# Sums of squares of the norms on TensorE: one column of ones as moving operand instead of 128

## The chip, the core and the metric

The kernel runs on one core of one Trainium2 chip, as one launch. The metric is the device time of that launch in microseconds (us). A core has five engines that work beside one another, each through its own instructions in their order: TensorE (PE, matrix products; the loading of its stationary operand is shown apart as PEld), VectorE (DVE), ScalarE (ACT), GpSimd (POOL) and SyncE (SP, which here only issues DMA transfers). They wait for one another through semaphores.

## The reference, cut to what matters

Two transformer layers over 512 tokens `x` and 256 context tokens `ctx`, of 1024 channels, and a last norm. Every norm is an RMS norm; the attention of layer 0 has one per head as well (`diff_out`).

```python
def rmsnorm(x, g):
    xf = x.astype(jnp.float32)
    y = xf * lax.rsqrt(jnp.mean(xf * xf, axis=-1, keepdims=True) + EPS)
    return (y * g.astype(jnp.float32)).astype(x.dtype)

def modulate(x, g, shift, scale):
    return rmsnorm(x, g) * (1 + scale) + shift

def diff_out(o, g, lam_init):
    b, t = o.shape[0], o.shape[1]
    return (rmsnorm(o, g) * (1.0 - lam_init)).reshape(b, t, B_V_WIDTH)

# reference(), one layer l
    a = modulate(h, norm1_g[l], sh1, sc1)
    ac = modulate(hc, norm1_g[l], csh1, csc1)
    ...                                      # l = 0: even_mixer, l = 1: odd_mixer
    h = h + g1 * y
    h = h + g2 * swiglu(modulate(h, norm2_g[l], sh2, sc2), ffn_w_in[l], ffn_w_out[l])
    ...                                      # the same for hc in layer 0
    return rmsnorm(h, final_g)
```

## The kernel before

**Layout.** Activations are kept transposed: eight tiles of 128 channels by tokens. Almost all time goes into large products, which are computed in three passes of a high and a low part (`mm3`, L106 to L108). A matmul of fp32 operands, as the norms use it, is shown as two records in the trace, each with its own weight load: two passes.

**One norm.** `squares` (L186) and code like it squares the channel tiles on ACT (L191) and adds them up on DVE (L193) to a tile `sq` of 128 partitions by T tokens, whose column sums are wanted. In the feed-forward parts some of the squares aren't added beforehand: they are handed over as a list `more` of further tiles (`sqs`), and TensorE adds them. `rstd_diag` (L145) then does the following.

- For each block of 128 tokens a matmul with the block of `sq` as the stationary operand (128 by 128) and `ones`, a 128 by 128 tile of ones, as the moving one (L156); for each tile of `more` the same again, added in PSUM (L161). Row p of the result is the sum of token p; all its 128 columns are equal.
- DVE reads one column of each block with a stride of 128 (`col`), scales it and adds EPS (L164, or L166 in the heads), and works out the reciprocal root in ten small instructions, L135 to L139, on 128 by 2 to 128 by 6 values.
- DVE writes for each block a diagonal matrix of these values (L173).

`spread` (L179) multiplies ones with the diagonals (L183), which puts the value of each token on all 128 partitions; DVE and ACT then modulate the activations with it (L199 to L201 in `modulate`).

**Where it is called.** At the start for `x` (four blocks), in the first projections for `ctx` (two blocks), in the four heads of layer 0's attention (`norm`, four and two blocks in each), before and within both feed-forward parts (`ffn_rstd` and `ffn`), before layer 1 for both streams (`modulated`, four and two blocks with four tiles of `more`), and at the end in two halves (`final_rows`, two blocks with three tiles of `more` each). In all there are 94 sum matmuls: 50 at L156 and 44 at L161, or 188 passes.

**The order of the work.** The program is written in Python as a sequence, and the framework's scheduler (`TileContext(..., schedule_with_timeline_sim=True)`, the last lines of the file) places the instructions of each engine by its own estimates of how long each takes. A different operand size can therefore move instructions that have nothing to do with the norms.

**Names of the places.** In the attention of layer 0, `qa`, `qb`, `kh` and `kl` are a head's queries and keys, `pw` their products in PSUM (L542, L543), `e` the exponentials (ACT, L546), `pb` from L564 their transposes, `ath` and `atl` the high and low part of these (L122, L123), which are multiplied with the values `vhi` and `vlo` by L106 to L108. Matmuls to `pf` from `ax` and a weight slot `w` are the gated projections of the other branch, which fill TensorE's time between. For layer 1, `w` is a weight slot: ACT writes its high part (L81) and POOL the low part (L84); `ax` are the high (ACT, L200) and low (DVE, L201) part of the normed activations; `pw` their product.

Of the kernel before, what the change touches and what calls it, by code (L numbers as in the profile page):

```python
# [14 lines left out]
P = 128  # L15
# [11 lines left out]
class Builder:  # L27
# [117 lines left out]
    def rstd_diag(self, accs, inv, bank=None, eps=None, at=None, more=()):  # L145

        nc = self.nc
        nb = sum(T for _, T in accs) // P
        ms = self.small(nb)
        o = 0  # L150
        for acc, T in accs:
            ps = (bank or self.bank)()
            n = T // P
            for j in range(n):
                c = slice(j * P, (j + 1) * P)
                self.last_sum = nc.tensor.matmul(ps[:, c], acc[:, c], self.ones, start=j == 0, stop=not more,  # L156
                                                 skip_group_check=True)
            for t in more:
                for j in range(n):
                    c = slice(j * P, (j + 1) * P)  # L160
                    nc.tensor.matmul(ps[:, c], t[:, c], self.ones, start=False, stop=t is more[-1], skip_group_check=True)  # L161
            col = ps[:, 0:T].rearrange("p (j f) -> p j f", f=P)[:, :, 0]
            if eps is None:
                nc.vector.tensor_scalar(ms[:, o:o + n], col, inv, EPS, ALU.mult, ALU.add)  # L164
            else:
                nc.vector.scalar_tensor_tensor(ms[:, o:o + n], col, inv, eps[:, o:o + n], ALU.mult, ALU.add)  # L166
            o += n
        r = self.rsqrt_small(ms, nb)
        dgs, o = [], 0
        for acc, T in accs:  # L170
            dg = at if at is not None else self.tmp()
            for j in range(T // P):
                self.last_diag = nc.vector.tensor_scalar(dg[:, j * P:(j + 1) * P], self.ident, r[:, o + j:o + j + 1], None,  # L173
                                                         ALU.mult)
            dgs.append(dg[:, :T])
            o += T // P
        return dgs
# [1396 lines left out]
```

## Time and profile before

| | us |
|---|---|
| median of three runs | 1590.26 |
| lowest and highest | 1588.08 and 1591.02 |
| the profiled execution, its own time | 1588.33 |
| its span in the trace | 1586.3 |
| ACT, POOL and DVE busy in the span | 723.3, 830.7 and 1084.7 |
| TensorE's mean granted clock, as a share of full speed | 0.988 |

Time is counted in the trace from the start of the span; 2.03 us of the execution's own time lie outside it (1588.33 less 1586.3). A row of the list of groups gives the line, the engine, the operation, the tiles written and read, the partitions and sizes, the count, the busy time and the mean duration of one, and behind the bar the idle time of the engine just before them. A row of the timeline gives the start, how long the run of equal instructions took, the engine and the line; in brackets stands how long the engine had been idle and what released it. The rows of stretches give for each engine its busy time, then the granted TensorE clock.

### The profile page before, as it was taken

To read this page: it belongs to the slowest core of one execution; us is meant where nothing else is said; L and a number is where in the kernel's file an instruction comes from. 1 tells how busy PE (TensorE), PEld (TensorE's weight loads), DVE (VectorE), ACT (ScalarE), POOL (GpSimd) and SP (SyncE) were. 2 spreads that over 40 slices of the span, in tenths; PEclk is the share of its full clock that TensorE was granted. 3 is DMA by queue.
4 is the path that set the end of the run, shared out by engine and by line. 5 is a ranking of instruction groups with operands and counts; after the bars stand their busy time and mean duration, and the time that the engine had idled before them with its cause. 6 is when DMAs were issued, how large, how long until landed. Compare 5 with 4: busy or idle time off the path is not lost.

```text
span 1586.3 us, 24984 instructions
## 1 busy us (share of the span) xinstructions
PE 1518.7 (96%) x9547; PEld 1352.2 (85%) x9547; DVE 1084.7 (68%) x1958; ACT 723.3 (46%) x1472; POOL 830.7 (52%) x565
## 2 busy tenths in 40 slices
PE   6999988999999999999999989999999999999996
PEld 4776877889989999999999978777869989999996
DVE  4720788765688788888785585765667976666656
ACT  2412676553552333333333244565655644444443
POOL 0463211061256776677676415531304398888883
PEclk9999999999999999999999999999999999999998
DMA  8845100033223333454451012110225132323301
GB/s 328 308 145 188 40 8 1 3 131 133 67 80 113 114 120 106 140 166 147 164 165 57 27 52 80 61 34 14 68 80 206 54 120 88 113 92 109 94 14 54
DMA packets 54295, 162.00 MB, mean 102 GB/s; under 512 B 6176, under 2 KB 10656, under 8 KB 46496
## 3 DMA queue, kind: packets, MB, share of 16 engines
q1 hardware_dynamic: 47120, 135.11, 25.5%
q10 hardware_dynamic: 7056, 25.30, 4.9%
q8 instruction: 75, 1.23, 0.3%
q14 instruction: 44, 0.36, 0.1%
HBM read 158.29 MB, written 2.10 MB: 101 GB/s over the span
## 4 chain that ended last, share of the span: by engine, by line
PE 83%; DVE 10%; ACT 3%; issue 2%; DMA 1%; POOL 0%; POOLq 0%; SPq 0%; DVEq 0%; ACTq 0%
PE pw L106 11%; PE pw L107 11%; PE pw L108 11%; PE pb L107 8%; PE pb L106 8%; PE pb L108 8%; PE pf L106 4%; PE pf L107 4%; PE pf L108 4%; PE pb L1427 2%; PE pb L1416 2%; PE pf L359 2%; PE pw L1379 1%; PE pw L1387 1%; PE pw L542 1%
## 5 line engine op out<-in xcount | busy, mean ns | idle before, releaser
L84 POOL TENSOR_TENSOR w<-raw,w 128x512 fp32r<-128x512 f32 (+1 forms) x84 | 127.5, 1525 | 242.9 <-ACT w L81 220.5
L107 PE MATMUL pw<-ax,w 128*128 128x384 f32 (+2 forms) x732 | 233.9, 320 | 3.7 <-DVE ax L201 2.3
L106 PE MATMUL pw<-ax,w 128*128 128x384 f32 (+2 forms) x732 | 232.9, 322 | 4.1 <-DVE q L879 1.9
L108 PE MATMUL pw<-ax,w 128*128 128x384 f32 (+2 forms) x732 | 233.1, 320 | 0.1
L774 DVE SCALAR_TENSOR_TENSOR xT<-pb,mod,xT 128x512 f32<-128x512 f32 (+3 forms) x208 | 145.7, 707 | 125.8 <-PE pb L108 125.5
L879 POOL TENSOR_TENSOR w<-raw,w 128x512 fp32r<-128x512 f32 x110 | 169.4, 1555 | 19.7 <-ACT w L879 19.5
L879 POOL TENSOR_TENSOR w<-t,w 128x512 fp32r<-128x512 f32 x99 | 148.6, 1504 | 55.6 <-ACT w L879 55.6
L106 PE MATMUL pb<-hh,w 128*128 128x512 f32 x480 | 171.0, 356 | 2.3 <-DVE xT L774 2.3
L108 PE MATMUL pb<-hh,w 128*128 128x512 f32 x480 | 171.5, 357 | 0.3 <-DVE w L879 0.3
L107 PE MATMUL pb<-hh,w 128*128 128x512 f32 x480 | 171.1, 356 | 0.0
L107 PE MATMUL pw<-T,w 128*128 128x384 f32 (+1 forms) x508 | 156.9, 310 | 1.2 <-DVE T L123 1.2
L106 PE MATMUL pw<-T,w 128*128 128x384 f32 (+1 forms) x508 | 156.3, 310 | 1.1 <-DVE hs L879 1.1
L108 PE MATMUL pw<-T,w 128*128 128x384 f32 (+1 forms) x508 | 157.0, 310 | 0.0
L106 PEld LDWEIGHTS pw<-ax,w 128*128 128x128 f32 x732 | 138.5, 190 | 12.5 <-DVE q L879 2.6
L107 PEld LDWEIGHTS pw<-ax,w 128*128 128x128 f32 x732 | 139.0, 190 | 11.2 <-DVE ax L201 3.6
L106 PE MATMUL pf<-ax,w 128*128 128x256 f32 (+2 forms) x420 | 139.9, 333 | 7.9 <-DVE qf L252 5.0
L108 PEld LDWEIGHTS pw<-ax,w 128*128 128x128 f32 x732 | 139.2, 190 | 3.1 <-DVE w L948 0.4
L107 PE MATMUL pf<-ax,w 128*128 128x256 f32 (+2 forms) x420 | 138.8, 330 | 0.0
L108 PE MATMUL pf<-ax,w 128*128 128x256 f32 (+2 forms) x420 | 138.7, 330 | 0.0
L879 POOL TENSOR_TENSOR hh<-hs,hh 128x768 fp32r<-128x768 f32 (+1 forms) x42 | 80.7, 1922 | 90.0 <-ACT hh L879 67.6
L879 POOL TENSOR_TENSOR w<-rawo,w 128x512 fp32r<-128x512 f32 x59 | 103.5, 1754 | 30.1 <-ACT w L879 30.1
L228 DVE SCALAR_TENSOR_TENSOR junk<-ar,cb 128x1024 bf16<-128x1024 f32 x64 | 105.6, 1651 | 0.0
(378 smaller groups left out, 3936.8 us busy)
## 6 DMA issues: line engine op xcount, KB each, us to landing
raw<-ffn_in SPq DMA_DIRECT2D x44, 1024.0 KB, 5.1
ar<-ada SPq DMA_DIRECT2D x24, 1024.0 KB, 6.9
ar<-ada ACTq DMA_DIRECT2D x48, 512.0 KB, 3.5
rawo<-ffn_out SPq DMA_DIRECT2D x88, 256.0 KB, 3.0
raw<-odd_out SPq DMA_DIRECT2D x32, 256.0 KB, 2.7
raw<-qk SPq DMA_DIRECT2D x16, 256.0 KB, 7.9
raw<-uv SPq DMA_DIRECT2D x16, 256.0 KB, 2.7
raw<-even_out SPq DMA_DIRECT2D x8, 512.0 KB, 3.5
```

What stands on the lines that cost most here:

```text
L84: eng.tensor_tensor(lo, raw, hi.bitcast(F32), ALU.subtract)
L106: mm(out, s[0], m[0], start=start, stop=False, **kw)
L107: mm(out, s[0], m[1], start=False, stop=False, **kw)
L108: return mm(out, s[1], m[0], start=False, stop=stop, **kw)
L228: return self.nc.vector.scalar_tensor_tensor(junk, t, 1.0, self.cb[who], ALU.mult, ALU.mult, accum_out=self.acc[who][:, col:col + 1])
L359: nc.tensor.matmul(ps[32 * q:32 * q + 32, :w], cst[:, k, :], t[:, w * q:w * q + w], start=k == 0, stop=k == KT - 1, skip_group_check=True)
L542: nc.tensor.matmul(ps[:, :TX], Q[c][:, qs], K[c][p][:, :TX], start=p == 0, stop=p == 1)
L774: ins = self.nc.vector.scalar_tensor_tensor(h, ps[:, r], self.modcol(l, j, m, who), h, ALU.mult, ALU.add)
L879: tail[key] = fn(*args, **kw)
L1379: nc.tensor.matmul(ps[:, st:en], Q, K[g][p][:, b0 * P:b1 * P], start=p == 0, stop=p == 1, skip_group_check=True)
L1416: last = nc.tensor.transpose(pt[:, x * P:(x + 1) * P], es[2 * (x % 2) + x // 2][:, kb * P:(kb + 1) * P], self.ident)
L1427: nc.tensor.matmul(po[64 * h:64 * h + 64, :], V[vb][:, 64 * g:64 * g + 64], t[:, h * TC:h * TC + TC], start=kb == 0, stop=kb == nb - 1, sk ...
```

## The change

In `rstd_diag` the moving operand of the sum matmuls is one column of the tile of ones. Each block of tokens then has one result column in PSUM, the j-th for block j, and DVE reads these adjacent columns in place of every 128th. The stationary operands, the number of matmuls, what DVE does with the sums and everything behind it stay. The rest of the file only moves down by a line from L162 on.

```diff
             for j in range(n):
                 c = slice(j * P, (j + 1) * P)
-                self.last_sum = nc.tensor.matmul(ps[:, c], acc[:, c], self.ones, start=j == 0, stop=not more,
-                                                 skip_group_check=True)
+                self.last_sum = nc.tensor.matmul(ps[:, j:j + 1], acc[:, c], self.ones[:, :1], start=j == 0,
+                                                 stop=not more, skip_group_check=True)
             for t in more:
                 for j in range(n):
                     c = slice(j * P, (j + 1) * P)
-                    nc.tensor.matmul(ps[:, c], t[:, c], self.ones, start=False, stop=t is more[-1], skip_group_check=True)
-            col = ps[:, 0:T].rearrange("p (j f) -> p j f", f=P)[:, :, 0]
+                    nc.tensor.matmul(ps[:, j:j + 1], t[:, c], self.ones[:, :1], start=False, stop=t is more[-1],
+                                     skip_group_check=True)
+            col = ps[:, 0:n]
```

The scheduler also places some instructions otherwise, in three places: the first products of the start, the attention heads of layer 0, and the passage from layer 0's feed-forward part to layer 1. Three pieces show it.

In the attention heads on PE, before (`pw` are products of queries and keys, `pb_1884` a product with the values):

```order
L542 MATMUL pw_2194<-kh_1834,qb_1823 128x512
L543 MATMUL pw_2194<-kh_1834,qb_1823 128x256
L542 MATMUL pw_2194<-kl_1835,qb_1823 128x512
L543 MATMUL pw_2194<-kl_1835,qb_1823 128x256
L107 MATMUL pb_1775<-atl_1812,vhi_1290 128x256
...
L564 MATMUL pb_1885<-ident_100,e_1871 128x128
L644 MATMUL pf_2792<-ident_100,f_354_1913 128x128 x2
L542 MATMUL pw_2287<-kh_1828,qa_1822 128x512
L543 MATMUL pw_2287<-kh_1828,qa_1822 128x256
L542 MATMUL pw_2287<-kl_1829,qa_1822 128x512
L543 MATMUL pw_2287<-kl_1829,qa_1822 128x256
L106 MATMUL pb_1884<-ath_1890,vhi_1290 128x256
```

And of the change, the same work:

```order
L107 MATMUL pb_1775<-atl_1812,vhi_1290 128x256
...
L565 MATMUL pb_1885<-ident_100,e_1871 128x128
L543 MATMUL pw_2194<-kh_1834,qb_1823 128x512
L544 MATMUL pw_2194<-kh_1834,qb_1823 128x256
L543 MATMUL pw_2194<-kl_1835,qb_1823 128x512
L544 MATMUL pw_2194<-kl_1835,qb_1823 128x256
L645 MATMUL pf_2792<-ident_100,f_354_1913 128x128 x2
L106 MATMUL pb_1884<-ath_1890,vhi_1290 128x256
...
L543 MATMUL pw_2287<-kh_1828,qa_1822 128x512
```

The products `pw_2194` go behind five products and four transposes, and the six matmuls of `pb_1884` that follow in the order go ahead of the products `pw_2287`.

Later in the same attention, on ACT, before (`e` are exponentials, `kh_2390` and `qb_2379` keys and queries of the next head):

```order
L546 ACTIVATE e_2408,sa_2403<-pw_2404,sa_2402 128x256
L645 COPY f_361_1976<-pf_2863 128x512
L546 ACTIVATE e_2414,sa_2403<-pw_2410,sa_2402 128x256
L276 COPY kh_2390<-f_141_889 64x768
L277 COPY kh_2390<-f_141_889 64x768
L262 ACTIVATE qb_2379<-f_139_885 64x768
L576 COPY o_2159<-pb_2207 128x256
```

And of the change:

```order
L646 COPY f_361_1976<-pf_2863 128x512
L547 ACTIVATE e_2408,sa_2403<-pw_2404,sa_2402 128x256
L577 COPY o_2159<-pb_2207 128x256
L277 COPY kh_2390<-f_141_889 64x768
L278 COPY kh_2390<-f_141_889 64x768
L263 ACTIVATE qb_2379<-f_139_885 64x768
L547 ACTIVATE e_2414,sa_2403<-pw_2410,sa_2402 128x256
```

The exponential `e_2414` now stands behind the three copies of keys and queries.

At the start of layer 1, on ACT, before (`w_9039` is the first weight slot, `ax_8730` and `ax_8732` the first two normed tiles):

```order
L787 ACTIVATE sqs_8809<-ctxT_640_3314 128x256
L81 COPY w_9039<-raw_9037 128x512
L200 ACTIVATE ax_8730<-t_8910,mod_69 128x512
L81 COPY w_9044<-raw_9042 128x512
L81 COPY w_9117<-raw_9115 128x512
L200 ACTIVATE ax_8732<-t_8914,mod_69 128x512
L200 ACTIVATE ax_8734<-t_8918,mod_69 128x512
```

And of the change:

```order
L788 ACTIVATE sqs_8809<-ctxT_640_3314 128x256
L201 ACTIVATE ax_8730<-t_8910,mod_69 128x512
L201 ACTIVATE ax_8732<-t_8914,mod_69 128x512
L81 COPY w_9039<-raw_9037 128x512
L81 COPY w_9044<-raw_9042 128x512
L201 ACTIVATE ax_8734<-t_8918,mod_69 128x512
L81 COPY w_9117<-raw_9115 128x512
```

The copy of the first weight slot goes behind two normed tiles, and with it POOL's low part of that slot (L84).

## The prediction

> **What bounds the kernel now.** I read the page first: the share of each engine, the granted clock, and the chain that ended last.
>
> ```profile
> PE 1518.7 (96%) x9547; PEld 1352.2 (85%) x9547; DVE 1084.7 (68%) x1958; ACT 723.3 (46%) x1472; POOL 830.7 (52%) x565
> ...
> PEclk9999999999999999999999999999999999999998
> ...
> PE 83%; DVE 10%; ACT 3%; issue 2%; DMA 1%; POOL 0%; POOLq 0%; SPq 0%; DVEq 0%; ACTq 0%
> ```
>
> TensorE is busy for 96% of the span and carries 83% of the chain, so time taken from TensorE is worth its full length where nothing else is late. DVE's 10% are short passages in which TensorE waits for a norm or a softmax. Next come the groups of the sum matmuls and of two weight loads, with shapes kept apart, because they say what one pass costs.
>
> ```profile
> L156 PE MATMUL pb<-ones,sq 128*128 128x128 f32 x74 | 11.3, 293 | 12.5 <-DVE sq L193 12.5
> L161 PE MATMUL pf<-ones,sqs 128*128 128x128 f32 x32 | 4.1, 275 | 0.0
> L161 PEld LDWEIGHTS pf<-ones,sqs 128*128 128x128 f32 x32 | 3.8, 192 | 0.0
> L359 PEld LDWEIGHTS pf<-ar,cst 128*32 128x32 f32 x256 | 5.5, 109 | 8.9 <-issue 6.5 <-DMA raw<-uv 0.4 <-PE pw L384 0.2
> ```
>
> The durations, 275 ns for a pass and 192 ns for its load, overlap and are not what a pass takes from TensorE. That is the step from one pass to the next in a run of them, in the timeline of the passage to layer 1:
>
> ```profile
> 922.41 1.64 PEld L161 LDWEIGHTS pf<-ones,sqs 128*128 128x128 f32 x14
> ...
> 922.52 1.73 PE L161 MATMUL pf<-ones,sqs 128*128 128x128 f32 x14
> ```
>
> Fourteen passes take 1.73 us from the first start to the last end. Less one duration that is 1.455 us for 13 steps, 0.112 us each; for the loads (1.64 - 0.192) / 13 = 0.111. In 188 passes the sums take about 21 us of TensorE's time, 1.3% of the run. That is all the change can touch directly.
>
> **What a pass with one column costs.** Two things run in each step: 128 columns stream through, and the next 128 by 128 weights are loaded. The change cuts the first to one column and leaves the second whole. So I need the weight load alone. From the two load groups above: 192 less 109 ns for 128 against 32 columns is 83 ns for 96 columns, 0.86 ns each, so 128 columns hold the load path for about 0.11 us and the rest of the 192 ns is latency that overlaps. The second look is a matmul of the mask in layer 1's attention (L1384), the nearest thing to a short moving operand behind a full weight load. Its operands are of the kind that streams twice as fast:
>
> ```profile
> 1028.41 0.19 PEld L1384 LDWEIGHTS pw<-mask,identr 128*128 128x128 f32 x1
> ...
> 1028.53 0.23 PE L1384 MATMUL pw<-mask,identr 128*128 128x128 f32 x1
> 1028.53 0.19 PEld L1387 LDWEIGHTS pw<-kh,qa 128*128 128x128 f32 x1
> ...
> 1028.64 0.19 PEld L1387 LDWEIGHTS pw<-kl,qa 128*128 128x128 f32 x1
> ...
> 1028.76 0.29 PE L1387 MATMUL pw<-kl,qa 128*128 128x256 f32 x1
> ```
>
> ```profile
> 1043.56 0.39 PE L106 MATMUL pf<-ax,w 128*128 128x512 f32 x1
> ...
> 1043.80 0.40 PE L107 MATMUL pf<-ax,w 128*128 128x512 f32 x1
> ```
>
> With 512 columns such a pass steps 0.24 us, so 128 columns stream in about 0.06. Yet the load behind the mask's matmul starts 0.12 us after the mask's own, and the one behind that 0.11 us later. Halving the stream did not shorten the step: the weight load holds it at 0.11. A one-column pass must still load its 128 columns, so it should step between 0.108 and 0.112 us. I take 0.109, the load's own time by the slope (0.86 x 128 is 0.110), and get 188 x 0.003 = 0.6 us less, with bounds of 0 and 188 x 0.004 = 0.75.
>
> [...]
>
> **The ends of the groups.** The last pass of a group has no load behind it, so there the missing stream counts in full: up to 0.11 us before DVE may read the sums. [...]
>
> ```profile
> 12.23 2.05 PE L156 MATMUL pb<-ones,sq 128*128 128x128 f32 x8 [12.23 <-DVE sq L193]
> ```
>
> ```profile
> 1570.64 1.50 PE L161 MATMUL pw<-ones,sqs 128*128 128x128 f32 x12
> ...
> 1571.79 0.48 DVE L173 TENSOR_SCALAR dg<-ident,sm 128x128 f32<-128x128 f32 x2
> 1572.19 0.15 DVE L164 TENSOR_SCALAR sm<-pw 128x2 f32<-128x2 f32 x1
> ...
> 1578.23 1.22 PE L183 MATMUL pf<-dg,ones 128*128 128x256 f32 x2 [5.20 <-DVE dg L173]
> ```
>
> At the end the sums stop at 1572.14 and DVE starts at 1572.19, so 0.1 us comes off the tail. At the start eight passes take 2.05 us, twice the rate of the fourteen above, so 0.2, in the shadow of the first products, which have other inputs. With the heads and layer 1 at 0.1 each the bound is 0.5; I take 0.4 less. What DVE reads keeps its count and its 2 to 4 values, 0.15 us each: nothing. The feed-forward groups between 306 and 920 us have TensorE full on both sides and gain only the 0.6 already counted:
>
> ```profile
> 306.00:920.00 614.00, 605.82 (x3481) 575.15 (x3480) 461.56 (x725) 238.46 (x449) 361.70 (x219) 1.00 0.34 112
> ```
>
> **What the scheduler moved.** DVE, POOL and TensorE do the same amounts. At the start two transposes go behind six filling products, with inputs that are there; I cost that at nothing, since those six would follow anyway, and at 12 passes of 0.112, 1.3 us, if the transposes were the last to be waited for. The heads:
>
> ```profile
> 249.61 0.50 PE L542 MATMUL pw<-kh,qa 128*128 128x512 f32 x1 [0.70 <-ACT e L546]
> ```
>
> ```profile
> 267.30 0.83 ACT L276 CAST kh<-f 64x768 fp32r<-64x768 f32 x1 [0.43 <-PE pw L543]
> ...
> 268.15 0.83 ACT L277 CAST kh<-f 64x768 fp32r<-64x768 f32 x1
> ...
> 269.01 0.84 ACT L262 ACTIVATE qb<-f 64x768 fp32r<-64x768 f32 x1
> ...
> 270.98 0.47 PE L542 MATMUL pw<-kh,qa 128*128 128x512 f32 x1 [1.66 <-ACT e L546]
> ...
> 273.42 0.47 PE L542 MATMUL pw<-kh,qb 128*128 128x512 f32 x1 [0.95 <-ACT e L546]
> ```
>
> The wait of 0.70 us is that of `pw_2287` for its slot; the six products now ahead of it cover it, so 0.7 less. Then the exponential `e_2414` stands behind three copies of 0.83, 0.83 and 0.84 us. Behind it wait the next products in its PSUM slot and all of TensorE's queue: up to 2.5 us more. What is late next gets easier, for the same copies caused the 1.66 and 0.95 us before. Bounds: 0.70 + 1.66 + 0.95 = 3.3 less if all three waits close, 2.5 more if none of them does. I take 0.7 less: the first is sure, and the new wait and the two old ones about cancel (2.5 against 2.6).
>
> At the start of layer 1:
>
> ```profile
> 930.00 0.60 ACT L81 CAST w<-raw 128x512 fp32r<-128x512 f32 x1
> ...
> 930.68 1.26 POOL L84 TENSOR_TENSOR w<-raw,w 128x512 fp32r<-128x512 f32 x1 [6.73 <-ACT w L81]
> 930.73 1.88 DVE L173 TENSOR_SCALAR q<-ident,sm 128x128 f32<-128x128 f32 x4
> ...
> 932.76 1.10 PE L183 MATMUL pf<-q,ones 128*128 128x512 f32 x2 [1.41 <-DVE sm L164]
> ...
> 934.68 0.72 ACT L200 ACTIVATE ax<-t,mod 128x512 fp32r<-128x512 f32 x1 [4.08 <-DVE t L199]
> ...
> 935.45 0.50 PE L106 MATMUL pw<-ax,w 128*128 128x512 f32 x1 [1.60 <-ACT ax L200]
> ```
>
> Four diagonals take 1.88 us here while POOL works beside, two took 0.48 in the tail; without POOL they take 0.96, and the spread comes 0.9 us earlier. But the slot's copy (0.60) now follows two tiles of 0.72 on ACT: 934.68 - 0.9 + 0.72 + 0.72 + 0.60 is 935.8 against 935.45, and POOL's low part ends 1.26 later. DVE's modulation runs 0.9 ahead and pays that back. I take nothing, with 0.9 less and 1.3 more as bounds.
>
> The sum is 0.6 + 0.4 + 0.7 = 1.7 us less. The profiled execution, 1588.33 with 2.03 of it outside the span, would become 1586.6. It lies 1.93 under the median of 1590.26; from that the same 1.7 gives **1588.6 us**.
>
> **The rivals.** *Passes that the load does not hold, faster.* If weights were loaded well ahead, a pass could cost what a load of 32 columns holds, 0.86 x 32, 0.027 us: 188 x 0.085 is 16 us less, 1574. The steps at 1028.41 to 1028.64 speak against it: no stream is in the way there and the loads are still 0.11 apart. [...] The mask's rows show a step of 0.11 to 0.12 instead.
>
> *The heads lose their fill, slower.* The exponential behind three copies holds TensorE for 2.5 us, and the two old waits stay since DVE is full there:
>
> ```profile
> 236.00:246.00 10.00, 7.36 (x28) 5.33 (x26) 8.54 (x22) 8.98 (x14) 1.82 (x1) 0.67 0.00 0
> ...
> 266.00:276.00 10.00, 7.39 (x51) 6.48 (x50) 9.92 (x33) 7.09 (x16) 2.72 (x2) 1.00 0.01 2
> ```
>
> DVE has 9.92 of these 10 us, so nothing can be caught up. Between 236 and 246 TensorE had been as idle as between 266 and 276, and its clock fell to 0.67: another 3.3 us of full clock. With 2.5 that is up to 5.8, less the sure 1.7: 4 more, 1594. It decides from the point where the new wait is not shorter than 1.66 + 0.95.
>
> *A pause mended, faster.* The same clock loss is there already at 236 to 246. If work moves so that such a slow stretch doesn't come, 3.3 go with the 1.7: 1585. Its stalls lie ahead of what was moved, so I give it little.
>
> *Short passes can't overlap their loads, slower.* Then each step is the load's whole 192 ns: 188 x 0.08 is 15 more, 1605. Against it stand the mask's rows again.
>
> *The change does nothing by itself* and the scheduler's moves alone count: 1588.6 + 1.0, within the forecast.
>
> **How the numbers follow.** The forecast's own range goes by the bounds: 0.75 + 0.5 + 3.3 + 0.9 less is 1584.8, 0.7 + 2.5 + 1.3 more is 1594.8. A measurement of this kernel tells about 0.2%, 3.2 us, from no change: faster is under 1587.1, slower over 1593.4. The forecast has 0.58: 0.36 within, 0.14 faster, 0.08 slower. Passes without hold 0.12 and a pause mended 0.05, faster; lost fill 0.20 and no overlap 0.05, slower. So faster 0.31, same 0.36, slower 0.33. The range, 1582 to 1596, takes in the heads' rival on top of the bounds and leaves out the two rivals on the passes.
>
> **What would show it.** Right: runs of L161 still step 0.11 us while their mean duration falls by about 0.1; the last L164 starts 0.1 us sooner after its group; TensorE's count of busy time falls by more than the time does. The wait at `pw_2287` is gone, a new one of some 2 us stands behind `e_2414`, and by 300 us both kernels are within 1 us of each other. Wrong: a step of L161 under 0.09 us or over 0.13, a shift of over 3 us between 245 and 305 or between 925 and 957, or a slow stretch of the clock that before did not have.

## The result and the profile after

The change made the kernel slower: a median of 1596.80 us (1593.02 to 1600.76, 8 runs) against 1589.17 us (1585.91 to 1591.02, 8 runs) for the kernel before, a ratio of 1.0043 with a 95% interval of 1.0034 to 1.0052. The forecast was 1588.6 us, its range ended at 1596. The profiled execution took 1593.02 us, with a span of 1591.2; it is the shortest of the eight, so its trace shows 4.7 of some 7 us (1593.02 less 1588.33).

The page of the change, with engine shares, granted clock and the chain that ended last:

```profile
PE 1525.7 (96%) x9547; PEld 1360.1 (85%) x9547; DVE 1080.2 (68%) x1958; ACT 723.2 (45%) x1472; POOL 832.0 (52%) x565
...
PEclk9999998999999999999999979999999999999998
...
PE 83%; DVE 9%; ACT 4%; issue 3%; POOL 1%; DMA 0%; SPq 0%; POOLq 0%; DVEq 0%; ACTq 0%
```

TensorE is busy 7 us longer, although its passes got shorter and their count is the same. The row of the clock says why: it has an 8 in the seventh slice and a 7 in the 24th, where before all slices but the last had a 9. The groups of the sum passes show the same:

```profile
L161 PE MATMUL pf<-ones,sqs 128*128 128x1 f32 x32 | 5.0, 280 | 0.0
L161 PE MATMUL pb<-ones,sqs 128*128 128x1 f32 x16 | 3.6, 343 | 0.0
L161 PE MATMUL pw<-ones,sqs 128*128 128x1 f32 x24 | 3.0, 247 | 0.0
```

The last group, at the end of the program, fell from 275 to 247 ns. The first two, in the passage to layer 1, rose above 275. The starts of the same matmul in both timelines tell where the time went; their difference, after less before, is called the shift from here on:

| matmul | before, us | after, us | after less before |
|---|---|---|---|
| heads, L107 `pb<-atl,vhi` | 247.32 | 245.37 | -1.95 |
| heads, L543 `pw<-kl,qa` | 297.60 | 301.59 | +3.99 |
| feed-forward, L108 `pb<-hh,w` | 474.47 | 477.09 | +2.62 |
| first sums for layer 1, L156 | 921.63 | 924.27 | +2.64 |
| layer 1, L108 `pb<-w,ax` | 963.83 | 970.69 | +6.86 |
| layer 1, L1387 `pw<-kh,qb` | 999.25 | 1004.48 | +5.23 |
| end of the span | 1586.3 | 1591.2 | +4.9 |

Two places lose: the heads 5.9 us between the first two rows, after they had gained 1.6 us from 225 us on, and the passage to layer 1 another 4.2 us. Parts of it come back, 1.1 us in a wait that was 2.26 us at 466.89 and is 1.20 us at 469.51, and 1.6 us around 985 us, where the kernel before had a stretch of halved clock (0.50 from 985.0 to 988.4 us) and this one has none.

In the heads, the waits behind the moved exponential (timeline of the change):

```profile
269.19 0.83 ACT L278 CAST kh<-f 64x768 fp32r<-64x768 f32 x1
270.04 0.84 ACT L263 ACTIVATE qb<-f 64x768 fp32r<-64x768 f32 x1
...
271.52 0.39 PE L544 MATMUL pw<-kh,qb 128*128 128x256 f32 x1 [2.45 <-DVE kl L280]
...
274.37 0.76 PE L543 MATMUL pw<-kh,qa 128*128 128x512 f32 x1 [1.54 <-ACT e L547]
```

and the stretches there (PE busy time first, then the other engines; the clock is the third number from the end):

```profile
266.00:276.00 10.00, 6.01 (x39) 5.19 (x39) 9.88 (x34) 6.67 (x16) 2.19 (x1) 0.86 0.01 2
276.00:286.00 10.00, 10.00 (x48) 8.77 (x48) 7.37 (x23) 2.85 (x6) 0.00 (x0) 0.80 0.00 1
```

The wait is 2.45 us, and the clock is halved just after it: 10.00 us of busy TensorE at 0.80. The row names DVE's `kl`, which ended at that very moment (270.57 and 0.95). The moved exponential, with the reading of its accumulator, ended 0.05 us before, and in a run below with the same wait it is the one that is named.

In the passage to layer 1, the stretches before:

```profile
924.00:931.00 7.00, 7.00 (x64) 7.00 (x63) 5.37 (x20) 2.99 (x7) 0.32 (x1) 1.00 0.45 142
931.00:937.00 6.00, 2.67 (x10) 1.26 (x9) 5.57 (x16) 2.32 (x4) 1.96 (x2) 1.00 0.14 44
937.00:944.00 7.00, 5.73 (x15) 3.99 (x14) 6.96 (x13) 3.09 (x6) 3.38 (x3) 0.51 0.36 112
944.00:951.00 7.00, 7.00 (x32) 5.81 (x32) 6.64 (x14) 3.24 (x6) 0.00 (x0) 1.00 0.01 2
```

and after:

```profile
924.00:931.00 7.00, 7.00 (x54) 7.00 (x52) 3.41 (x8) 2.47 (x6) 0.72 (x1) 0.82 0.32 87
931.00:937.00 6.00, 6.00 (x29) 6.00 (x30) 3.85 (x18) 1.25 (x3) 0.00 (x0) 0.50 0.19 66
937.00:944.00 7.00, 4.57 (x12) 2.73 (x13) 4.40 (x10) 3.08 (x6) 1.68 (x2) 0.50 0.00 0
944.00:951.00 7.00, 7.00 (x21) 5.35 (x22) 7.00 (x12) 3.16 (x6) 3.54 (x3) 0.64 0.36 112
```

Before, the clock halved at 937 us, after a wait of TensorE (2.67 us busy of 6). After, it halved while TensorE's row says busy without a gap: 7.00 of 7.00. What ran there were one-column passes (timeline of the change):

```profile
924.27 0.95 PE L156 MATMUL pf<-ones,sq 128*128 128x1 f32 x8
925.09 1.70 PE L161 MATMUL pf<-ones,sqs 128*128 128x1 f32 x14
...
928.03 2.97 PE L161 MATMUL pf<-ones,sqs 128*128 128x1 f32 x16
...
934.91 2.70 PE L161 MATMUL pb<-ones,sqs 128*128 128x1 f32 x12
```

The fourteen passes still step some 0.11 us (1.70 less a duration of about 0.25, over 13), as forecast. The sixteen step 0.17 (2.97 less 0.35, over 15), in part at half the clock, and the twelve, wholly at half the clock, 0.21.

So two theories stand. **Gate**: passes that stream one column in a step of 0.11 us, which had held 128, leave TensorE's array almost empty while its queue is full, and the clock is granted by what the array does. **Order**: the moved instructions cost everything, and the halved clock is a consequence of where they were put.

### The profile page after: what moved, and what is told of

Same layout as the page of the kernel before. It is cut to its first block, busy times and chain, and to the rows that moved or that the text cites. A ratio compares the mean times of both kernels' runs of the same rounds, so it can differ in the third digit from the quotient of the medians.

```text
span 1591.2 us, 24986 instructions
## 1 busy us (share of the span) xinstructions
PE 1525.7 (96%) x9547; PEld 1360.1 (85%) x9547; DVE 1080.2 (68%) x1958; ACT 723.2 (45%) x1472; POOL 832.0 (52%) x565
## 4 chain that ended last, share of the span: by engine, by line
PE 83%; DVE 9%; ACT 4%; issue 3%; POOL 1%; DMA 0%; SPq 0%; POOLq 0%; DVEq 0%; ACTq 0%
PE pw L106 11%; PE pw L108 11%; PE pw L107 11%; PE pb L106 8%; PE pb L107 8%; PE pb L108 8%; PE pf L106 4%; PE pf L107 4%; PE pf L108 4%; PE pb L1428 2%; PE pb L1417 2%; PE pf L360 2%; PE pw L1380 1%; PE pw L1388 1%; PE pw L543 1%
## 5 line engine op out<-in xcount | busy, mean ns | idle before, releaser
L84 POOL TENSOR_TENSOR w<-raw,w 128x512 fp32r<-128x512 f32 (+1 forms) x84 | 127.7, 1529 | 242.8 <-ACT w L81 220.5
L107 PE MATMUL pw<-ax,w 128*128 128x384 f32 (+2 forms) x732 | 233.4, 320 | 1.8 <-DVE ax L467 1.4
L108 PE MATMUL pw<-ax,w 128*128 128x384 f32 (+2 forms) x732 | 233.5, 320 | 0.4 <-POOL w L84 0.3
L108 PE MATMUL pb<-hh,w 128*128 128x512 f32 x480 | 171.5, 357 | 0.3 <-DVE w L880 0.3
L107 PE MATMUL pb<-hh,w 128*128 128x512 f32 x480 | 171.1, 356 | 0.0
L107 PE MATMUL pw<-T,w 128*128 128x384 f32 (+1 forms) x508 | 157.0, 310 | 1.2 <-DVE T L123 1.2
L108 PE MATMUL pw<-T,w 128*128 128x384 f32 (+1 forms) x508 | 157.0, 310 | 0.0
L107 PEld LDWEIGHTS pw<-ax,w 128*128 128x128 f32 x732 | 139.1, 190 | 9.1 <-DVE ax L467 2.2
L108 PEld LDWEIGHTS pw<-ax,w 128*128 128x128 f32 x732 | 139.0, 190 | 3.9 <-POOL w L84 1.0
L107 PE MATMUL pf<-ax,w 128*128 128x256 f32 (+2 forms) x420 | 138.3, 329 | 0.0
L108 PE MATMUL pf<-ax,w 128*128 128x256 f32 (+2 forms) x420 | 138.1, 329 | 0.0
```

The lines of the kernel that those rows point to most:

```text
L84: eng.tensor_tensor(lo, raw, hi.bitcast(F32), ALU.subtract)
L107: mm(out, s[0], m[1], start=False, stop=False, **kw)
L108: return mm(out, s[1], m[0], start=False, stop=stop, **kw)
```

## The experiments

To part the two, the order of one kernel was imposed on the other: after the program is written, each instruction of an engine gets an edge of issue order alone to its predecessor in the other kernel's order. What these edges cost by themselves does not show: two runs below with the order of before, with 64 columns and with 128 in layer 1, came to 1.0005 of the time before (0.9996 to 1.0013 in both).

```diff
+def pin(tc):
+    import base64, json, zlib
+    traced = list(tc.nc.cur_bb.bb.instructions)
+    dep = mybir.DependencyInfo(mybir.DependencyClass.NoSync, mybir.DependencyReason.DATA)
+    for _, deltas in json.loads(zlib.decompress(base64.b85decode(ORDER))):
+        at, last = 0, None
+        for d in deltas:
+            at += d
+            if last is not None:
+                tc.add_manual_dep(traced[at], traced[last].name, dep, reason="pin")
+            last = at
...
 def body(tc, a):
     Builder(tc, a).build()
+    pin(tc)
```

`ORDER` is the list of positions for each engine, in a line of its own that is left out here. Ratios are to the kernel before, measured beside each group of runs, with 95% intervals. They are the ones on record and differ from the quotient of the two medians by up to 0.12%.

**One column, order of before.** The kernel of the change with `pin`.

> The change's one-column passes, with every engine's instructions in the order that the kernel before has. Two theories share the 7 us. Gate: in the passage to layer 1 (from about 921 us) the one-column passes keep TensorE's queue full but its array nearly empty, and the clock is halved by them; then the halved stretch at 924 to 940 us appears here too, with no wait of TensorE ahead of it, the heads (226 to 306 us) stand as before, and the time is 3 to 5 us above the kernel before. Order only: the moved instructions cost everything, the clock at 924 to 931 us stays at 1.00, and the time is 0.5 to 1.5 us below the kernel before. A halved stretch in the heads of over 14 us in all would speak for a third cause.

1597.07 us, ratio 1.0038 (1.0024 to 1.0051): as slow as the change, without any moved instruction. The stretches of this run:

```profile
924.00:931.00 7.00, 7.00 (x56) 7.00 (x56) 3.95 (x10) 2.47 (x6) 0.72 (x1) 0.88 0.23 74
931.00:937.00 6.00, 6.00 (x31) 6.00 (x29) 4.02 (x15) 1.75 (x4) 1.26 (x1) 0.50 0.23 82
```

The clock halves again with TensorE's queue full. Order as the whole cause falls. What was not expected is a halved stretch in the heads from 274 to 281 us in this execution, with the order of before, and with it a loss of 3.2 us between 225 and 306 us. Of the five executions on record with the order of before and other column counts, two lose 3.2 us in the heads against the trace of before, one 1.9, one 0.2 and one nothing. The trace of the change loses 4.3 between the same points, so its loss there can't be put down to the order alone; what the order costs is read from the times below.

**128 columns, order of the change.** The kernel before with `pin`.

> The kernel before, 128 columns in each pass, with every engine's instructions in the order of the change. Gate: no halved stretch at 924 to 931 us, since the passes are long; the heads keep the 2.4 us wait behind the moved exponential and the halved stretch after it, so the shift against the kernel before is 4 to 6 us at 300 us and stays there: 3 to 6 us slower. Order only: the whole 7 us, with the halved stretch from about 928 us too.

1591.89 us, ratio 1.0011 (0.9999 to 1.0023). No halved clock at 924 to 931 us. In the heads the wait of 2.45 us (at 271.61) is there and a shift of 4 us at 300 us, as in the change, but the median lies less above before than expected: the shift is down to 1.3 us at 999 us, since layer 1 has one halved stretch of 3.4 us here where the trace of before has 6.8. (This execution loses 3.6 us again later, in halved stretches of 6.8 us at 1183 and 3.4 us at 1275 us.)

**One column but in layer 1, order of before.**

```diff
     def modulated(self, l, sq, off, n, more):
+        self.sum_w = P
         r = self.rstd_rows(sq[:, off:off + n], n, 1.0 / D, self.bank if off == TX else self.fill, None, more)
+        self.sum_w = 1
```

with `sum_w` columns in `rstd_diag` in place of one.

> One column everywhere but in layer 1's norms (modulated), which keep 128; the order of the kernel before. Gate: no halved stretch at 924 to 931 us, and what the short passes give shows: 0.5 to 1.5 us below the kernel before, 4 to 6 us below the run with one column everywhere in this order. If short passes cost time in other places as well (starts, heads, feed-forward parts), it stays above the kernel before by more than 1 us.

1590.94 us, ratio 1.0005 (0.9996 to 1.0013), and the clock stays at 1.00:

```profile
924.00:931.00 7.00, 7.00 (x63) 7.00 (x63) 4.24 (x14) 2.72 (x8) 0.73 (x1) 1.00 0.41 128
```

One column in the other passes, 188 less 60, is worth nothing that can be measured, and the 60 of layer 1 carry the loss: 1.0038 against 1.0005. The gain of 0.5 to 1.5 us was a miss.

**Layer 1 alone with one column, order of before.** The same two lines with the widths exchanged.

> One column in layer 1's norms alone, 128 everywhere else, in the order of the kernel before. Gate: the halved stretch from about 926 us is there, some 20 us long in place of the 7 us from 937, and the time is 4 to 7 us above the kernel before, all of it arising between 924 and 950 us. If the short passes elsewhere carry the cost, within 1.5 us of the kernel before.

1592.92 us, ratio 1.0022 (1.0014 to 1.0031), some 3.5 us; the clock halves from 927.2 us, and the shift grows from 0.2 us at 921 to 1.7 at 929 and 3.1 at 945. It is a little less than expected. In this execution some 3.4 us at full clock lay between two halved stretches (0.76, 0.76 and 0.50 in the three stretches from 924 to 944 us), where the run with one column everywhere had none.

**64 and 32 columns everywhere, order of before** (`sum_w = 64`, `sum_w = 32`).

> 64 columns in every sum pass, in the order of the kernel before. The step should stay 0.11 us, held by the weight load. Gate, if it goes by the share of time in which columns stream: a run of such passes streams about half of the time, and with the full products between them the stretch at 921 to 931 us stays above half, so the clock stays at 1.00 and the time is within 1.5 us of the kernel before. If the gate goes by another measure than streamed columns, the halved stretch comes as with one column, 3 to 5 us slower.

> 32 columns in every sum pass, in the order of the kernel before. The step stays 0.11 us, so TensorE's array streams about a quarter of the time within such a run. Gate by streamed share: in the 3.4 us from 924.3 to 927.6 us some 70% are sum passes, so the share streamed falls to about 0.3 + 0.7 x 0.25, near one half: the halved stretch may come or not; if it comes, 3 to 6 us slower, as with one column; if not, within 1.5 us of the kernel before, as with 64.

1591.53 us, 1.0005 (0.9996 to 1.0013), and 1591.20 us, 1.0014 (1.0003 to 1.0024). With 64 columns the clock from 924 to 937 us is 1.00, with TensorE full in the first seven of these. With 32 the profiled execution is 7.6 us late here, so its sums run from 929.3 to 938.9 us, and the clock is 1.00 there too:

```profile
928.00:931.40 3.40, 3.40 (x30) 3.28 (x29) 2.28 (x5) 1.88 (x4) 0.54 (x1) 1.00 0.02 5
931.40:934.80 3.40, 3.40 (x32) 3.40 (x31) 2.18 (x5) 1.23 (x3) 0.19 (x1) 1.00 0.29 91
```

So a quarter of the columns is enough in this place, where full products stand between the groups. The run with 32 is still a little slower than before, and its profiled execution, 1597.30 us, is the slowest of its twelve: it has halved stretches in the heads (3.4 us from 235.1, 6.8 from 245.4 and 6.8 from 276.1 us), at 474 us (3.4 us) and behind the sums (10.2 us from 941.7 us), after waits of TensorE. Whether the short passes had a part in these stays open.

**The gate by itself.** Both theories so far were weighed at one place. Here the norm ahead of layer 0's feed-forward part sums each block twelve times, and takes a twelfth, in a stretch where TensorE never waits; both runs have the same order. The columns of all other sums are 128; the twin has 128 in the second line added as well.

```diff
     def ffn_rstd(self, sq, rest, NH=TA // 2):
-        self.r = self.rstd_rows(sq[:, :NH], NH, 1.0 / D, self.fill, None, rest)
+        m = 12 if NH == TA // 2 else 1
+        self.sum_w = 1 if m > 1 else P
+        self.r = self.rstd_rows(sq[:, :NH], NH, 1.0 / (m * D), self.fill, None, list(rest) + [sq[:, :NH]] * (m - 1))
+        self.sum_w = P
```

> The kernel before, but the norm ahead of layer 0's feed-forward part sums each block twelve times (72 passes, with the mean taken of twelve sums) with one column each, in a stretch where TensorE never waits; the same order as its twin with 128 columns. Gate: some 3.4 us after the first of these passes (about 383 us) the clock halves with no idle time of TensorE before it, for two windows of 3.4 us or more, and the time is 3 to 6 us above the twin. If the halved clock at 924 us came from something else there than short passes, the clock stays 1.00 at 383 to 395 us and the two are equal within 1.5 us, or this one is faster by up to 72 x 0.004 us.

> The twin: the same 72 passes with 128 columns each. The clock stays 1.00 from 370 to 400 us by either theory, and the time is that of the kernel before plus the 54 to 66 added passes of 0.112 us: 6 to 8 us above it.

1600.73 us, 1.0078 (1.0063 to 1.0093), and with 128 columns 1597.07 us, 1.0048 (1.0034 to 1.0062). The run with one column, timeline and stretches:

```profile
379.81 0.72 PE L158 MATMUL pf<-ones,sq 128*128 128x1 f32 x6
380.39 12.22 PE L163 MATMUL pf<-ones,sq 128*128 128x1 f32 x66
```

```profile
374.00:381.00 7.00, 7.00 (x47) 7.00 (x45) 1.75 (x4) 1.05 (x2) 0.00 (x0) 1.00 0.01 2
381.00:384.40 3.40, 3.40 (x25) 3.40 (x24) 0.00 (x0) 0.00 (x0) 0.00 (x0) 0.73 0.00 0
384.40:388.00 3.60, 3.60 (x19) 3.60 (x19) 0.00 (x0) 0.00 (x0) 0.00 (x0) 0.50 0.00 0
...
395.00:399.00 4.00, 4.00 (x22) 4.00 (x21) 0.49 (x3) 0.00 (x0) 0.00 (x0) 0.84 0.00 0
```

And its twin:

```profile
382.03 7.53 PE L163 MATMUL pf<-ones,sq 128*128 128x128 f32 x66
```

```profile
384.40:388.00 3.60, 3.60 (x35) 3.60 (x34) 0.00 (x0) 0.00 (x0) 0.00 (x0) 1.00 0.00 0
```

This is the clearest row of the study. TensorE and its weight loads are busy for every moment of it; with 128 columns the clock stays 1.00 and 66 passes take 7.53 us, with one column it is 0.50 and they take 12.22 us. In these two executions the run with one column is 1.5 us ahead of its twin at 279 us and 4.9 us behind it at 396; the medians differ by 3.7. The trace is one of each kernel and there are four times of each, but the same halving stands in every one of the four traces with passes of one column in a dense run, and in none of their counterparts with 128. That the clock is halved by short passes with TensorE's queue full is shown.

**Both at once.** The change's order, one column, but 128 in layer 1.

> The change with its own order of instructions, but 128 columns in layer 1's norms; one column everywhere else. It completes a square: order of before or of the change, layer 1 with long or short passes. If the two causes simply add, the moved instructions cost here what they cost with 128 columns throughout (0.0 to 0.2% above the kernel before), and the change itself is 3 to 6 us above this run. If they don't add (the stretch that the heads lose is given back or lost again at layer 1), this run is within 2 us of the change.

1594.66 us, ratio 1.0018 (1.0006 to 1.0030). Order alone costs 0.11 and 0.18% in the two runs that have it with long passes in layer 1, the short passes there 0.22 to 0.33%; together about the 0.43% measured. They add within the intervals, which are wide: of this run's eleven times three lie at 1587.7 to 1589.3 us, as fast as the kernel before, and eight at 1592.3 to 1596.6.

**The heads alone.** The kernel before, of whose order only the heads are replaced by the change's.

> The kernel before with 128 columns, in which only the attention heads of layer 0 (some 196 to 305 us) have the change's order; start and layer 1 as before. If the heads carry what the moved instructions cost: the wait of 2.4 us behind the exponential that follows the three copies, a halved stretch right after it, a shift of 2 to 5 us at 300 us, and 0.1 to 0.25% above the kernel before. If the loss lies at the start or at layer 1: within 1 us at 300 us and in the time.

1589.91 us, ratio 1.0013 (1.0001 to 1.0024). The wait and the shift (3.0 us at 301 us) are those of the change:

```profile
270.90 0.39 PE L543 MATMUL pw<-kh,qb 128*128 128x256 f32 x1 [2.45 <-ACT e L546]
```

TensorE's waits of over 0.3 us in 226 to 306 us add up to 9.9 us against 8.5 before, and the clock is halved from 272 to 279 us. But these waits add up to as much, 9.9 us, in the run with one column and the order of before. The ratio is close to that of the whole order (0.13 against 0.11 and 0.18%), so most of what the order costs seems to arise here, though the lower end of the interval is near nothing.

**The exponential put back.** The same, with ACT in the order of before from that exponential on.

> The same with one thing undone: from the exponential e_2408 on, ACT has the order of the kernel before, so that e_2414 stands ahead of the three copies again. If that wait is what costs: the shift at 300 us falls to between -1.5 and +1 us and the halved stretch after 271 us is gone. If the products that were moved cost by themselves, the shift stays 2 to 5 us.

1596.86 us, ratio 1.0043 (1.0030 to 1.0057): a miss in both directions. TensorE's order had been made for the other order of ACT, and now waits once for long:

```profile
274.81 0.58 PE L106 MATMUL pb<-ath,vhi 128*128 128x256 f32 x1 [5.95 <-ACT ath L122]
```

One wait of 5.95 us replaces the two of 2.45 and 1.20. The wait behind the copies is thus not one instruction in a wrong place: in this pair of orders, putting that one back made it worse. Which of the moved products is to blame stays open.

**Feeding the array.** If the clock follows what streams, work that nobody reads should hold it through a wait.

```diff
+    def feed(self, out, n):
+        new = [self.nc.tensor.matmul(out[:, :P], self.ones, self.ones, start=True, stop=True, skip_group_check=True).ins
+               for _ in range(n)]
+        self.extra = list(self.extra) + ([new] if n else [])
+
     def spread(self, dg, bank=None, keep=0):
         out = (bank or self.bank)()
+        self.feed(out, keep)
...
-                    nc.vector.scalar_tensor_tensor(c, c, self.subg, self.spread(dg), ALU.mult, ALU.mult)
+                    r = self.spread(dg, None, 10 if t == 0 and off == 0 else 0)
+                    nc.vector.scalar_tensor_tensor(c, c, self.subg, r, ALU.mult, ALU.mult)
...
             ps = self.wide()
+            self.feed(ps, 7 if n == 0 else 0)
```

`extra` tells `pin` where the added matmuls stand; all others keep the order of before.

> The kernel before, in its order, with work for TensorE that nobody reads in two of its waits: ten matmuls of ones with ones (128 columns) ahead of the first head's spread (wait of 2.64 us at 241.58) and seven ahead of layer 1's first product (1.60 us at 935.45), each into the bank that the next matmul overwrites. Gate: the halved stretches from 240.9 and 937.2 us shrink or vanish, and the time falls by 1 to 5 us where TensorE sets the pace behind them. If the halving there has another cause, or DVE sets the pace, the time stays within 1 us or rises by up to 1 us, where the added work outlasts the wait.

1586.48 us, ratio 0.9981 (0.9972 to 0.9989): faster than both kernels. Stretches of the kernel before and of this run:

```profile
240.00:248.00 8.00, 6.42 (x18) 4.53 (x19) 7.82 (x20) 5.01 (x8) 1.15 (x1) 0.57 0.00 0
```

```profile
240.00:248.00 8.00, 6.08 (x39) 4.65 (x38) 7.95 (x21) 6.27 (x12) 1.81 (x1) 1.00 0.01 2
...
937.00:944.00 7.00, 6.50 (x28) 5.30 (x29) 6.89 (x13) 3.37 (x5) 1.78 (x1) 1.00 0.30 101
```

The clock is 1.00 where it was 0.57 and, at 937 to 944 us, 0.51. Against the trace of before it gains 1.3 us between 225 and 247 us and 2.1 us between 929 and 945, at the two places that were fed; it is 1.9 us ahead at 476 us and 4.0 us ahead at 945 us. A halved stretch at 1268 us, which the trace of before does not have, takes 1.5 us of that back.

## Why the prediction was wrong

**The step that failed** is the price of a one-column pass: "it should step between 0.108 and 0.112 us. I take 0.109", and 0.6 us less as the whole direct effect. The step itself was right, at full clock: 0.112 us measured. But it was taken at the clock that the kernel before had been granted, and TensorE's full queue was taken for a busy TensorE. The trace of before couldn't show the difference, since every pass in it streamed 128 columns or more; the profile did show that the clock is granted stretch by stretch (0.67 between 236 and 246 us, 1.00 between 266 and 276), and how thin the streaming becomes in 60 such passes between 921 and 931 us could have been worked out. No term and no rival had a halved clock without a pause of the queue. What the runs showed in its place: the 60 passes of layer 1 halve the clock and cost 0.22 to 0.33%, 3.5 to 5 us, where some tenths of a microsecond had been forecast as gain.

**The ends of the groups**: 0.4 us less was forecast, at some 0.1 us for each end, because the stream of 128 columns was counted in full. Where DVE waits for a sum at full clock, it starts 0.313 us after the last pass does before (379.60 and 379.92 us) and 0.288 us after (383.28 and 383.57): 0.025 us for each end. At the program's end DVE has other work and starts no sooner: the sums stop at 1576.93 us, L174 takes 0.48 us from 1576.70, and L165 starts at 1577.10. The sign that the mean duration of L161 falls by about 0.1 us failed in the same way: outside layer 1 its groups fell from 275 and 274 ns to 247 and 239. With one column everywhere but in layer 1 the ratio is 1.0005 (0.9996 to 1.0013). By the forecast the 128 short passes of that run and their ends would give some 0.7 us less, 0.9996, at the very edge of the interval.

**The heads**: 0.7 us less was forecast. The wait of `pw_2287`, called sure to close, is still 0.65 us (at 250.83), since the exponential that frees its slot ends later too (at 250.77 us in place of 249.55). The new wait is 2.45 us as worked out (2.5), but it doesn't cancel with the old ones: 2.45 and 1.54 stand against 1.66 and 0.95. The halved stretch after them is what the rival *The heads lose their fill* had named, which put it at 4 us above for the whole. It stands there, for two pieces of 3.4 us each, in all four traces that have the change's order in the heads; of six with the order of before, two have two such pieces, two have one and two none. This rival, given 0.20, thus had a real wait and a real loss of clock, but its size was too large and the loss is not the new order's alone: measured by itself it is worth 0.13% (0.01 to 0.24).

**Layer 1**: nothing was forecast for what moved there, with bounds of 0.9 less and 1.3 more. In the run with 128 columns and the change's order the shift falls from 2.5 us at 929 to 1.8 us at 964, and in the change with 128 columns in layer 1 it is 1.9 us at both, as forecast. The 4.2 us lost there in the change come from the passes.

**The rival without a hold by the load** is refuted, as the rows of the mask's matmul had said: the step of a one-column pass at full clock is 0.112 us and not 0.027. *Short passes can't overlap their loads* is refuted as well by the same 0.112, against some 190 ns for one load.

**The range**: the sum of the upper bound has a term of 0.7 us that is worked out nowhere. The start's bound of 1.3 in its place makes it 1595.4 and not 1594.8, still below the 1596 where the range ends.

**What would show it**: the list named a slow stretch of the clock that before did not have. It stood there as a mishap that would upset the forecast, without a place or a price. Of the other signs, the step of 0.11 us at full clock and the new wait of some 2 us came; the wait at `pw_2287` did not go, and at 300 us the kernels were 4.0 us apart and not within 1.

## What to carry to other kernels

TensorE's row in the profile said here that its queue was busy, not that columns streamed through its array: it had 3.60 of 3.60 us with the clock at 1.00 and at 0.50. Where passes with few moving columns come in a dense run, it pays to count what streams in each stretch of 3.4 us: here the full clock stayed after a stretch with full products in 0.41 of it, and was halved after those with 0.36 and 0.18. Cutting 128 equal columns to one gained nothing that shows, because the step stayed at 0.112 us, and cost 3.5 to 5 us in clock. The reverse paid: matmuls that nobody reads, issued into a bank about to be overwritten, kept the clock at 1.00 through two waits, where it had been 0.57 and 0.51, and made the kernel 0.19% faster. And one trace of each kernel is too few to price a wait: the same order lost between nothing and 3.2 us in the heads from one execution to the next.

## What the runs showed of the hardware

The halved clock came and went in pieces of 3.4 us: in the trace of before the halved stretches up to 1570 us last 6.8, 6.8, 6.8, 3.4 and 3.4 us, in that of the change 6.8, 6.8, 6.8, 20.5 and 3.4. In the run with 72 passes of one column it is halved from 382.6 to 396.3 us, 13.7 us or four such pieces, while the short passes last from 379.8 to 392.6: it begins after one piece that held mostly short passes (full products in 0.18 of it), and ends after one that held none. TensorE's row is full from 374 to 399 us.

The run with one column in layer 1 alone shows the pieces one by one:

```profile
920.40:923.80 3.40, 3.40 (x29) 3.26 (x27) 2.42 (x5) 1.88 (x4) 0.40 (x1) 1.00 0.03 5
923.80:927.20 3.40, 3.40 (x32) 3.40 (x31) 2.18 (x5) 1.23 (x3) 0.33 (x1) 1.00 0.27 77
927.20:930.60 3.40, 3.40 (x17) 3.40 (x18) 1.60 (x7) 0.83 (x2) 0.00 (x0) 0.50 0.64 214
930.60:934.10 3.50, 2.35 (x22) 2.26 (x20) 3.03 (x11) 0.93 (x2) 1.26 (x1) 0.99 0.00 0
934.10:937.50 3.40, 2.04 (x2) 0.50 (x2) 2.05 (x10) 0.18 (x1) 0.00 (x0) 0.50 0.23 77
```

The first had some 0.41 of its time in full products, by the starts of the matmuls, and the clock stayed; the second had 0.36 and the third was halved; the third held products almost throughout and the clock came back; the fourth held little but short passes and a pause, and the clock halved again. In the change, the piece ahead of the first halved one, 925.1 to 928.5 us, had 0.36 as well; sixteen short passes in 1.7 us at 410 us, half a piece, had no effect.

The same count can be made for waits: the share of a piece in which TensorE had matmuls, each from its start to the next one's or to its own end, with a pass of one column taken as 1/128 of one with 128. In the traces of before and of the change, between 22 and 1570 us, it is 0.27 to 0.45 in the ten pieces at full clock with a halved one behind them, and at least 0.49 in every one with another at full clock behind it. Of the halved pieces there, the ten with the full clock behind them had 1.00, and those with another halved one at most 0.87. These are estimates from the traces, for the ends of the matmuls are modelled. They give no sharp limit: in the run with one column but in layer 1, TensorE's row is busy for 0.62 of the time from 227.8 to 231.2 us, and the clock is halved behind it.

The pieces don't stand at the same place in every execution: in traces with the same order the first halving in the heads begins at 230.6, 231.2, 234.4 or 235.1 us. By the author's estimate this goes far to explain the spread, for the same wait may then fill one piece or be shared by two. In these four traces (before, one column but in layer 1, 64 and 32 columns) the halved time up to 1570 us is 27.3, 27.3, 34.1 and 44.4 us, and the times are 1588.33, 1589.64, 1592.85 and 1597.30 us: half of the 17.1 us between the ends is 8.5 us, and they are 9.0 apart. The kernel before itself ranges from 1585.67 to 1594.88 us in 29 runs.

At half the clock the weight load slows too: the 16 loads of L161 at 934.9 to 939.8 us of the change last 334 ns each, against 191 at the end of the program. The step does as well: 12.22 us for 66 passes, of which some 19 ran ahead of the halving at 0.112 us and the last lasts 0.35, leaves some 9.7 us for 46 steps, or 0.21 us a pass, nearly twice the 0.112.
